# Token-stationary merge blocks with a transpose back, and delays counted from the moment of adding, in a one-core decoder trunk

## The chip, the cores and the metric

The kernel runs on one core of a Trainium2 chip. The metric is the device time of one execution in microseconds (us). A core has TensorE (PE in the views; its weight loads are PEld), VectorE (DVE), ScalarE (ACT), GpSimd (POOL) and SyncE (SP). SP issues nearly all DMAs, POOL a few. Each has its own queue of instructions; a wait holds back all that stands behind it in that queue.

## The reference, cut to what matters

D_MODEL is 2048, there are 256 tokens and one layer. The layer is `h = x + Mixer(RMSNorm(x))`, then `h = h + SwiGLU(RMSNorm(h))`, then a last norm. The part that the change touches is the end of the mixer:

```
branch_a = (o * jax.nn.silu(r)) @ w_o_gla
...
u = jax.nn.silu(_layernorm(u, conv_norm_g, conv_norm_b))
branch_b = u @ w_pw2 + b_pw2
g_a, g_b = jnp.split(gates, 2, axis=-1)
merged = jax.nn.sigmoid(g_a) * branch_a + jax.nn.sigmoid(g_b) * branch_b
return merged @ w_out
```

`gates` is a slice of the input projection `h @ w_in`, as are the conv branch's inputs, q, k, v and r. All is float32.

## The kernel before, in words

Every float32 weight is split on the fly: ACT rounds a tile to `hi` (line 194) and DVE makes `lo = raw - hi` (line 196). A product is three products of such halves. Activations are split in the same way and kept as `[128, 512]` tiles: 256 tokens of the high half beside 256 of the low half, with channels on the partitions.

The mixer is a list of blocks, each 2048 input channels by 512 output channels (`add_block`, `run_blocks`). A block has 16 input tiles of 128 (index k), handled two at a time: a chunk, so 8 chunks in a block. There are two forms for a block:

- Form M (lines 243 and 244): the weights are stationary and the tokens stream. For each k and each of four groups of 128 output channels there is one matmul of `wh` with both halves of x (512 columns) and one of `wl` with the high half (256 columns). That is 8 matmuls for each k. The result has channels on the partitions, and its two halves have to be added (`merged_sum`: an ACT copy and a DVE addition of 256 columns).
- Form A (lines 235 to 237): the tokens are stationary and the weights stream. For each k and each of two groups of 128 tokens there are three matmuls of 512 columns, 6 for each k. The result has tokens on the partitions and needs no addition.

Both forms stream 3072 columns for each k. The order of blocks is: conv values and gates (8 blocks), a small block, k and q (4), v (4, the only ones in form A), r (4), gate a `ga` (4), gate b `gb` (4), `o` (4), `pw` (4), `out` (4). Then comes the feed-forward part, which is form A throughout (lines 1248 to 1250), with its order on the engines kept as written.

The weights of chunk c+4 are cast and subtracted while chunk c is multiplied (`LOOK` is 4; there are five `hi` and `lo` buffers and three raw buffers of 1 MB). All of it comes from one list of loads on SP.

Two queues of small steps run in the background: `conv_w_` (convolution and its layer norm) and `gla_w_` (the linear attention). `pump` is called once after each chunk. It advances a counter of chunks (`tick`) and issues steps while a budget lasts, `gla_w_` first. A step may carry a delay in chunks, which is counted from the queue's last step. `drain` issues whatever is still missing.

SBUF comes from pools. `pers` holds the scaled inputs `xs`, then the merged tiles `mgs`, then in the feed-forward part the residual `htk` and the hidden tiles `hsh` and `hsl`. `apool` and `tpool` serve the mixer. They are closed just ahead of the first `out` block and their space is opened again as `fpool` and `xpool`. At the start of each `out` block, `out_before` issues two loads of the residual `xr`, 256 KB each, on SP; the end of the block adds them (line 728).

At the very start, the first block takes eight single k, each with a 256 KB weight load and a 128 KB load of x.

Of the kernel before, what the change touches and what calls it, by code (L numbers as in the profile page):

```python
# [8 lines left out]
F32 = mybir.dt.float32  # L9
F32R = mybir.dt.float32r  # L10
# [14 lines left out]
LOOK = 4  # L25
RAW = 3
NA = 44
NPERS = 16
NF = 39
NX = 6  # L30

# [10 lines left out]
def trunk(ctx: ExitStack, tc, xT, par, convw, ws, wal2, nfin, out):  # L42
# [25 lines left out]
        return tpool.tile([P, T], F32, tag="t", name=nm(s))  # L68

    def ptile(dt=F32, s="p"):  # L70
        return pers.tile([P, NB], dt, tag="p", name=nm(s))

    def misc(shape=(P, 512)):
        return pacc.tile(list(shape), F32, tag="acc", name=nm("m"))
# [39 lines left out]
    class Work:  # L114
# [3 lines left out]
            self.steps, self.last = deque(), 0  # L118

        def add(self, cost, fn, delay=0):  # L120
            self.steps.append((cost, fn, delay))

        def mark(self, name):
# [32 lines left out]

    blocks = []

    def add_block(width, nk, form, xs, evac, before=None, budget=BUD):
        blocks.append(dict(width=width, nk=nk, form=form, xs=xs, evac=evac,  # L160
                           before=before, budget=budget))

    loads = []
    staged = {}
# [38 lines left out]
    def run_blocks():  # L203
        group = 0
        for b in blocks:
            b["first"] = len(loads)
            kp = 2 * NB // b["width"]
            b["chunks"] = [(k, kp) for k in range(0, b["nk"], kp)]
            if b is blocks[0]:
                b["chunks"] = [(k, 1) for k in range(NS)] + b["chunks"][NS // 2:]  # L210
            for k, kp in b["chunks"]:
                at = k * b["width"]
                loads.append((group + at // (4 * NB), at % (4 * NB), kp * b["width"], k, kp, b["width"]))
            group += b["nk"] * b["width"] // (4 * NB)
        for b in blocks:
            if b["before"]:
                b["before"]()
            nch = len(b["chunks"])
            nt = b["width"] // P if b["form"] != "A" else 2
            acc = {}  # L220

            def part(c, n):
                hi, lo = staged[b["first"] + c]
                if c == 0:
                    acc[n] = pacc.tile([P, NB], F32, tag="acc", name=nm("acc"))
                a = acc[n]
                k0, kp = b["chunks"][c]
                for kk in range(kp):
                    k = k0 + kk
                    st, en = k == 0, k == b["nk"] - 1  # L230
                    x = b["xs"]()[k]
                    if b["form"] == "A":
                        xh, xl = x[n] if isinstance(x, list) else (
                            x[:, i * T + n * P:i * T + (n + 1) * P] for i in range(2))
                        pe.matmul(a, lhsT=xh, rhs=hi[:, kk, :], start=st, stop=False)  # L235
                        pe.matmul(a, lhsT=xh, rhs=lo[:, kk, :], start=False, stop=False)  # L236
                        last = pe.matmul(a, lhsT=xl, rhs=hi[:, kk, :], start=False, stop=en)  # L237
                    else:
                        xh, xl = x[:, 0:T], x[:, T:2 * T]
                        wh = hi[:, kk, n * P:(n + 1) * P]  # L240
                        wl = lo[:, kk, n * P:(n + 1) * P]
                        if b["form"] == "M":
                            pe.matmul(a, lhsT=wh, rhs=x, start=st, stop=False)  # L243
                            last = pe.matmul(a[:, T:2 * T], lhsT=wl, rhs=xh, start=False, stop=en)  # L244
                        else:
                            a1 = a[:, 0:T]
                            pe.matmul(a1, lhsT=wh, rhs=xh, start=st, stop=False)
                            pe.matmul(a1, lhsT=wh, rhs=xl, start=False, stop=False)
                            last = pe.matmul(a1, lhsT=wl, rhs=xh, start=False, stop=en)
                order["p"] = last.ins  # L250
                if c == nch - 1:
                    b["evac"](n, acc.pop(n))

            for c in range(nch):
                while nload[0] + halves[0] <= b["first"] + c + LOOK:
                    load_next()
                for n in range(nt):
                    part(c, n)
                del staged[b["first"] + c]
                pump(b["budget"])  # L260
# [69 lines left out]

    def x_scaled(k):
        def f():
            s = ptile(F32R, "xs")
            t = ttile("xn")
            v.scalar_tensor_tensor(t, in0=xp[k // 2][:, k % 2, :], scalar=pcol(P_MIX, k), in1=rstd,
                                   op0=ALU.mult, op1=ALU.mult)
            split(s, t)
            X.append(s)
        return f
# [336 lines left out]


    SGA, SGB = {}, {}
    MG = {}
    XR = {}  # L680
    H2 = {}
    Y2 = []
# [2 lines left out]
    HTK = {}  # L685
    sums = {}

    def o_evac(blk):
        def f(n, a):
            i = 4 * blk + n  # L690
            t = merged_sum(a)
            g = SGA[i // 2][:, i % 2, :]
            v.tensor_tensor(g, t, g, op=ALU.mult)
        return f

    def pw_evac(blk):
        def f(n, a):
            i = 4 * blk + n
            t = merged_sum(a, pcol(P_PB, i))
            u = ttile("mg")  # L700
            v.tensor_tensor(u, t, SGB[i // 2][:, i % 2, :], op=ALU.mult)
            w = ttile("mg2")
            v.tensor_tensor(w, u, SGA[i // 2][:, i % 2, :], op=ALU.add)
            MG[i] = ptile(F32R, "mgs")
            split(MG[i], w)
        return f

    def out_before(blk):
        def f():
            if blk == 0:  # L710
                mx.close()
                es = ctx.enter_context
                ffn["f"] = es(tc.tile_pool(name="fpool", bufs=NF, reuse_waits="tile"))
# [347 lines left out]
    def back(blk, n, x):  # L1061
# [7 lines left out]
            later(0.7, lambda: cut(m), 0.2)  # L1069

        def cut(m):
            hi, lo = HSV[blk, n] = ptile(F32R, "hsh"), ptile(F32R, "hsl")
            cast(hi, m)
            sub(lo, m, hi)
            if blk not in HORDER[:2]:
# [23 lines left out]
    def h2_turn(th, nb):  # L1099
        def f():  # L1100
            m = misc()
            for q in range(4):
                i = 4 * nb + q
                kp(pe.transpose(m[:, q * P:(q + 1) * P], H2[i // 2][:, i % 2, th * P:(th + 1) * P], ident))
            HTK[th, nb] = ptile(s="htk")
            kp(sc.copy(HTK[th, nb], m))
        return f

# [180 lines left out]
    rk = pair_evac(SR, AF.Silu, "sr", after=lambda h: (gla_out(h), gla_gate(h)))  # L1289
    for blk in range(4):  # L1290
        add_block(NB, KT, "M", xx, rk(blk))
    ga = pair_evac(SGA, AF.Sigmoid, "sga")
    for blk in range(4):
        add_block(NB, KT, "M", xx, ga(blk), before=layernorm if blk == 0 else None)
    gb = pair_evac(SGB, AF.Sigmoid, "sgb")
    for blk in range(4):
        add_block(NB, KT, "M", xx, gb(blk))
    for blk in range(4):
        add_block(NB, KT, "M", lambda: OG, o_evac(blk),
                  before=(lambda: gla_w_.drain(("gla", 3))) if blk == 0 else None, budget=BO)  # L1300
    for blk in range(4):
        add_block(NB, KT, "M", lambda: US, pw_evac(blk),
                  before=(lambda: conv_w_.drain("conv")) if blk == 0 else None)
    for blk in range(4):
        add_block(NB, KT, "M", lambda: MG, out_evac(blk), before=out_before(blk))
    g0[0] = sum(b["nk"] * b["width"] for b in blocks) // (4 * NB)
    run_blocks()
    run_ffn()
# [59 lines left out]
```

## Time and profile before

| | us |
|---|---|
| median of 3 runs | 1654.43 |
| lowest and highest of the 3 | 1652.99, 1657.53 |
| the profiled execution | 1652.06 |
| its span, first to last instruction | 1650.3 |
| PE busy in the span | 1635.4 |
| DVE busy | 1397.8 |
| ACT busy | 930.4 |

The profile is one execution apart from the three runs. Its span is 1.8 us shorter than its own time. Busy time of PE counts matmuls whose ends are modelled and which overlap, so the pace of PE is read from when matmuls start, not from how long one lasts.

### The profile page before, as it was taken

The page shows a single profiled execution, that of the slowest core. Times are in us where ns is not written, and L with a number is a line of the kernel's source. Part 1 is how long each engine was busy: PE and PEld are TensorE (multiplying, and loading weights), DVE is VectorE, ACT ScalarE, POOL GpSimd, SP SyncE. Part 2 cuts the span into 40 slices and gives each one's busy share as a digit, 9 for nine tenths or more (in the row PEclk, how much of TensorE's full clock was granted, in tenths as well). Part 3 has the DMA queues.
Part 4 walks back from the last instruction along what each step waited for, and adds up shares of the span by engine and source line. Part 5 has one row for each costly group of instructions (what it writes and reads, how often), then busy time and mean ns, then how long its engine had stood idle before and what let it go on. Part 6 is the DMA issues. An engine that isn't in the chain of part 4 may idle for free.

```text
span 1650.3 us, 22488 instructions
## 1 busy us (share of the span) xinstructions
PE 1635.4 (99%) x8397; PEld 1391.0 (84%) x8397; DVE 1397.8 (85%) x2104; ACT 930.4 (56%) x1276; POOL 23.9 (1%) x46
## 2 busy tenths in 40 slices
PE   9999999999999999999999999999999999999997
PEld 8888888888888888888888788888888888888886
DVE  7998999888888889887668878888888899788876
ACT  6654444666667655476445565555555555454554
POOL 0000000000000000000000000000000000000000
PEclk9999999999999999999999999999999999999999
DMA  8555545554454445545555456666666666886963
GB/s 292 197 194 194 182 185 195 181 179 176 179 179 158 175 179 180 194 163 208 199 193 210 159 192 218 228 230 230 229 229 224 219 222 218 298 286 218 322 227 113
DMA packets 78365, 340.54 MB, mean 206 GB/s; under 512 B 8976, under 2 KB 10256, under 8 KB 58160
## 3 DMA queue, kind: packets, MB, share of 16 engines
q1 hardware_dynamic: 75232, 329.61, 57.2%
q0 software_dynamic: 2880, 9.44, 1.7%
q8 instruction: 65, 1.06, 0.3%
q14 instruction: 44, 0.36, 0.1%
q10 hardware_dynamic: 144, 0.07, 0.0%
HBM read 327.54 MB, written 11.53 MB: 205 GB/s over the span
## 4 chain that ended last, share of the span: by engine, by line
PE 96%; DVE 2%; ACT 1%; DMA 1%; issue 0%; SPq 0%; ACTq 0%; DVEq 0%
PE acc L243 32%; PE acc L244 16%; PE m L1249 13%; PE m L1250 13%; PE m L1248 13%; PE acc L235 2%; PE acc L237 2%; PE acc L236 2%; DVE lo L826 1%; PE m L1068 1%; DMA xr<-in_xT_dram 0%; PE m L596 0%; PE m L511 0%; DMA x<-in_xT_dram 0%; PE m L633 0%
## 5 line engine op out<-in xcount | busy, mean ns | idle before, releaser
L194 ACT CAST hi<-raw 128x1024 fp32r<-128x1024 f32 (+1 forms) x326 | 338.9, 1041 | 343.9 <-PE acc L243 287.8
L196 DVE TENSOR_TENSOR lo<-raw,hi 128x1024 fp32r<-128x1024 f32 (+1 forms) x326 | 394.3, 1210 | 110.3 <-ACT hi L194 107.7
L243 PE MATMUL acc<-xs,hi 128*128 128x512 f32 x1280 | 452.4, 398 | 0.0
L826 DVE TENSOR_TENSOR lo<-raw,hi 128x1024 fp32r<-128x1024 f32 x264 | 317.9, 1222 | 80.3 <-ACT hi L823 79.8
L244 PE MATMUL acc<-xs,lo 128*128 128x256 f32 x1280 | 359.0, 280 | 0.0
L823 ACT CAST hi<-raw 128x1024 fp32r<-128x1024 f32 x264 | 270.6, 1050 | 155.4 <-PE m L1250 81.9
L243 PEld LDWEIGHTS acc<-xs,hi 128*128 128x128 f32 x1280 | 240.3, 188 | 57.9 <-issue 0.3
L244 PEld LDWEIGHTS acc<-xs,lo 128*128 128x128 f32 x1280 | 241.8, 189 | 0.1
L393 DVE SCALAR_TENSOR_TENSOR yc<-u,cw,yc 128x255 f32<-128x255 f32 (+14 forms) x480 | 200.4, 467 | 0.1
L1248 PE MATMUL m<-hi,y2s 128*128 128x512 f32 x404 | 158.9, 393 | 1.6 <-ACT hi L823 1.6
L1249 PE MATMUL m<-lo,y2s 128*128 128x512 f32 x404 | 157.4, 390 | 0.8 <-DVE lo L826 0.8
L1250 PE MATMUL m<-hi,y2s 128*128 128x512 f32 x404 | 157.4, 390 | 0.0
L243 PE MATMUL acc<-xu,hi 128*128 128x512 f32 x256 | 90.9, 399 | 2.2 <-DVE xu L107 2.2
L1248 PEld LDWEIGHTS m<-hi,y2s 128*128 128x128 f32 x404 | 75.9, 188 | 17.3 <-ACT hi L823 2.1
L243 PE MATMUL acc<-ogs,hi 128*128 128x512 f32 x256 | 89.9, 395 | 0.0
L1249 PEld LDWEIGHTS m<-lo,y2s 128*128 128x128 f32 x404 | 75.9, 188 | 16.2 <-DVE lo L826 1.1
L1250 PEld LDWEIGHTS m<-hi,y2s 128*128 128x128 f32 x404 | 75.8, 188 | 15.9
L243 PE MATMUL acc<-us,hi 128*128 128x512 f32 x256 | 88.8, 391 | 0.0
L243 PE MATMUL acc<-mgs,hi 128*128 128x512 f32 x256 | 88.8, 391 | 0.0
L1249 PE MATMUL m<-lo,hr 128*128 128x512 f32 x216 | 84.2, 390 | 0.7 <-DVE lo L826 0.7
L1248 PE MATMUL m<-hi,hr 128*128 128x512 f32 x216 | 84.0, 389 | 0.0
L1250 PE MATMUL m<-hi,hr 128*128 128x512 f32 x216 | 84.0, 389 | 0.0
(256 smaller groups left out, 2790.6 us busy)
## 6 DMA issues: line engine op xcount, KB each, us to landing
raw<-in_weights_dram SPq DMA_DIRECT2D x157, 1024.0 KB, 4.8
raw<-in_weights_dram SPq DMA_DIRECT2D x268, 512.0 KB, 4.9
hr<-hsd SPq DMA_DIRECT2D x56, 256.0 KB, 6.5
hsd<-hsh POOLq DMA_DIRECT2D x18, 256.0 KB, 2.6
hsd<-hsl POOLq DMA_DIRECT2D x18, 256.0 KB, 3.0
raw<-in_weights_dram SPq DMA_DIRECT2D x8, 256.0 KB, 4.9
xr<-in_xT_dram SPq DMA_DIRECT2D x8, 256.0 KB, 5.4
out_dram<-fin SPq DMA_DIRECT2D x8, 256.0 KB, 3.1
```

What stands on the lines that cost most here:

```text
L194: order["a"] = sc.copy(fl(hi), r).ins
L196: order["v"] = v.tensor_tensor(fl(lo), r, fl(hi).bitcast(F32), op=ALU.subtract).ins
L235: pe.matmul(a, lhsT=xh, rhs=hi[:, kk, :], start=st, stop=False)
L236: pe.matmul(a, lhsT=xh, rhs=lo[:, kk, :], start=False, stop=False)
L243: pe.matmul(a, lhsT=wh, rhs=x, start=st, stop=False)
L244: last = pe.matmul(a[:, T:2 * T], lhsT=wl, rhs=xh, start=False, stop=en)
L393: v.scalar_tensor_tensor(y[:, d:T], in0=u_tile(i)[:, 0:T - d], scalar=cw[:, i, CW - 1 - d:CW - d], in1=y[:, d:T], op0=ALU.mult, op1=ALU.add)
L823: kp(sc.copy(dst, src))
L826: kp(v.tensor_tensor(dst, src, hi.bitcast(F32), op=ALU.subtract))
L1248: kp(pe.matmul(a, lhsT=xh, rhs=wh, start=st, stop=False))
L1249: kp(pe.matmul(a, lhsT=xh, rhs=wl, start=False, stop=False))
L1250: kp(pe.matmul(a, lhsT=xl, rhs=wh, start=False, stop=en))
```

## The change

The 16 blocks `ga`, `gb`, `o` and `pw` go from form M to form A, so their results have tokens on the partitions.

- `sg_evac`: the sigmoid of a gate is taken by ACT straight from the accumulator, 512 columns at a time, two instructions for a block instead of four groups of three.
- `o_evac`: one DVE multiplication of 512 columns for each token group.
- `pw_evac`: the bias now runs along the columns, so it is loaded as a tile that is the same on all partitions (`BP`, one 256 KB load on SP for each `pw` block). The source is a small DRAM tile `brow`, which one POOL DMA fills at the start of the program: 2048 values are read from the packed parameters with the two dimensions exchanged. DVE then adds the bias, multiplies by gate b and adds the gated branch a.
- `turn_merged`: `out` needs channels on the partitions. For each `pw` block, two groups of four 128x128 PE transposes are put into `gla_w_`, each with an ACT copy and a DVE subtraction of 512 columns that split the result into a pair of `mgs` tiles.
- `Work.add`: when the queue is empty, its first step's delay is counted from the moment of adding.
- `out_before` of the first `out` block runs ahead of its seventh chunk (`late`) and not ahead of the block, since the mixer's pools are still needed by the transposes.
- `pers` has 8 tiles of twice the size instead of 16; `xs`, `mgs`, `htk` and the pair of hidden halves are cut from them.

```
-NPERS = 16
+NPERS = 8
...
+        return pers.tile([P, 2, NB], dt, tag="p", name=nm(s))
+    pair_of = {}
+    def phalf(i, dt=F32, s="p"):
+        if i % 2 == 0:
+            pair_of[s] = ptile(dt, s)
+        return pair_of[s][:, i % 2]
...
         def add(self, cost, fn, delay=0):
+            if not self.steps:
+                self.last = tick[0]
             self.steps.append((cost, fn, delay))
...
             for c in range(nch):
+                if c == nch - 2 and b["late"]:
+                    b["late"]()
...
+    class Merged(dict):
+        def __missing__(self, k):
+            gla_w_.drain(("mg", k // 4))
+            return self[k]
+    MG = Merged()
+    BP = {}
+    brow = dpool.tile([16, P], F32, tag="brow", name="brow")
+    with nc.allow_non_contiguous_dma(reason="2048 values once"):
+        nc.gpsimd.dma_start(brow, par[:, P_PB:P_PB + 16].rearrange("p i -> i p"))
+    def sg_evac(store):
+        def mk(blk):
+            def f(n, a):
+                store[n, blk] = atile([P, NB], s="sg")
+                sc.activation(store[n, blk], a, AF.Sigmoid)
...
     def o_evac(blk):
         def f(n, a):
-            i = 4 * blk + n
-            t = merged_sum(a)
-            g = SGA[i // 2][:, i % 2, :]
-            v.tensor_tensor(g, t, g, op=ALU.mult)
+            g = SGA[n, blk]
+            v.tensor_tensor(g, a, g, op=ALU.mult)
+    def pw_before(blk):
+        def f():
+            if blk == 0:
+                conv_w_.drain("conv")
+            BP[blk] = atile([P, NB], s="bp")
+            nc.sync.dma_start(BP[blk], brow[4 * blk:4 * blk + 4, :].rearrange("a b -> (a b)").partition_broadcast(P))
     def pw_evac(blk):
         def f(n, a):
-            i = 4 * blk + n
-            t = merged_sum(a, pcol(P_PB, i))
-            u = ttile("mg")
-            v.tensor_tensor(u, t, SGB[i // 2][:, i % 2, :], op=ALU.mult)
-            w = ttile("mg2")
-            v.tensor_tensor(w, u, SGA[i // 2][:, i % 2, :], op=ALU.add)
-            MG[i] = ptile(F32R, "mgs")
-            split(MG[i], w)
+            u = SGB[n, blk]
+            t = atile([P, NB], s="mg")
+            v.tensor_tensor(t, a, BP[blk], op=ALU.add)
+            v.tensor_tensor(u, t, u, op=ALU.mult)
+            v.tensor_tensor(u, u, SGA[n, blk], op=ALU.add)
+            if n == 1:
+                for z in range(2):
+                    turn_merged(blk, z)
+                gla_w_.mark(("mg", blk))
+    def turn_merged(blk, z):
+        st = {}
+        def t():
+            m = st["m"] = misc()
+            for j in range(2):
+                for n in range(2):
+                    pe.transpose(m[:, (2 * j + n) * P:(2 * j + n + 1) * P],
+                                 SGB[n, blk][:, (2 * z + j) * P:(2 * z + j + 1) * P], ident)
+        def cut():
+            mg = ptile(F32R, "mgs")
+            m = st["m"].rearrange("p (k t) -> p k t", k=2)
+            sc.copy(mg[:, :, 0:T], m)
+            v.tensor_tensor(mg[:, :, T:2 * T], m, mg[:, :, 0:T].bitcast(F32), op=ALU.subtract)
+            for j in range(2):
+                MG[4 * blk + 2 * z + j] = mg[:, j]
+        gla_w_.add(0.0, t, 1 if z else 3)
+        gla_w_.add(0.7, cut, 1)
...
             if blk == 0:
+                gla_w_.drain(("mg", 3))
                 mx.close()
...
-    ga = pair_evac(SGA, AF.Sigmoid, "sga")
+    ga, gb = sg_evac(SGA), sg_evac(SGB)
     for blk in range(4):
-        add_block(NB, KT, "M", xx, ga(blk), before=layernorm if blk == 0 else None)
-    gb = pair_evac(SGB, AF.Sigmoid, "sgb")
+        add_block(NB, KT, "A", xx, ga(blk), before=layernorm if blk == 0 else None)
     for blk in range(4):
-        add_block(NB, KT, "M", xx, gb(blk))
+        add_block(NB, KT, "A", xx, gb(blk))
     for blk in range(4):
-        add_block(NB, KT, "M", lambda: OG, o_evac(blk),
+        add_block(NB, KT, "A", lambda: OG, o_evac(blk),
...
-        add_block(NB, KT, "M", lambda: US, pw_evac(blk),
-                  before=(lambda: conv_w_.drain("conv")) if blk == 0 else None)
+        add_block(NB, KT, "A", lambda: US, pw_evac(blk), before=pw_before(blk))
     for blk in range(4):
-        add_block(NB, KT, "M", lambda: MG, out_evac(blk), before=out_before(blk))
+        add_block(NB, KT, "M", lambda: MG, out_evac(blk), **{"before" if blk else "late": out_before(blk)})
```

## Rows read from the trace of the kernel before

**Rows 1.** The page's span, busy times, and the granted TensorE clock in 40 slices.
```profile
span 1650.3 us, 22488 instructions
PE 1635.4 (99%) x8397; PEld 1391.0 (84%) x8397; DVE 1397.8 (85%) x2104; ACT 930.4 (56%) x1276; POOL 23.9 (1%) x46
...
PEclk9999999999999999999999999999999999999999
```

**Rows 2.** The page's chain that ended last, shares by engine.
```profile
PE 96%; DVE 2%; ACT 1%; DMA 1%; issue 0%; SPq 0%; ACTq 0%; DVEq 0%
```

**Rows 3.** Waits of PE, whole span: us in total, times, longest.
```profile
PE acc L243 <- DVE xu L107: 2.2, 2, 1.2
PE m L1248 <- ACT hi L823: 1.6, 1, 1.6
PE m L1249 <- DVE lo L826: 1.5, 2, 0.8
```

**Rows 4.** One source line's matmuls in a stretch: count, ns each, first and last start.
```profile
L243 PE MATMUL acc<-xs,hi x199: 395/398/403, 591.7 to 661.7; 128*128 128x512 f32 x199
...
L243 PE MATMUL acc<-xs,hi x68: 391/391/478, 557.9 to 583.9; 128*128 128x512 f32 x68
...
L235 PE MATMUL acc<-hi,xs x63: 389/389/397, 288.8 to 331.0; 128*128 128x512 f32 x63
```

**Rows 5.** Matmuls of line 243 by the tile they read: stages o, pw, out.
```profile
L243 PE MATMUL acc<-ogs,hi x256: 391/391/582, 664.5 to 754.4; 128*128 128x512 f32 x128
...
L243 PE MATMUL acc<-us,hi x256: 391/391/391, 754.8 to 843.2; 128*128 128x512 f32 x128
...
L243 PE MATMUL acc<-mgs,hi x256: 391/391/391, 843.5 to 931.9; 128*128 128x512 f32 x128
```

**Rows 6.** Timeline of PE in stage o: start, duration, line.
```profile
698.08 0.40 PE L243 MATMUL acc<-ogs,hi 128*128 128x512 f32 x1
...
698.44 0.59 PE L428 MATMUL m<-lf,ones 128*128 128x256 f32 x2
```

**Rows 7.** Timeline of PE around four transposes in the feed-forward part.
```profile
960.09 0.39 PE L1250 MATMUL m<-hi,dy 128*128 128x512 f32 x1
960.32 0.60 PE L1104 MATMUL m<-ident,h 128*128 128x128 f32 x4
960.67 0.48 PE L1248 MATMUL m<-hi,y2s 128*128 128x512 f32 x1
...
961.22 0.39 PE L1250 MATMUL m<-hi,y2s 128*128 128x512 f32 x1
```

**Rows 8.** Windows at the start: length, busy us by engine, granted clock, DMA share, GB/s.
```profile
4.00:18.20 14.20, 13.22 (x66) 11.37 (x65) 10.62 (x26) 7.51 (x16) 0.00 (x0) 1.00 0.95 312
18.20:21.00 2.80, 1.61 (x10) 1.14 (x9) 1.69 (x3) 2.48 (x4) 0.00 (x0) 1.00 0.86 340
```

**Rows 9.** DMA queue of the parameters from 0 to 8 us: packets, MB, share of 16 engines.
```profile
q10 hardware_dynamic: 144, 0.07, 2.8%
```

**Rows 10.** The page's DMA queues, whole span, same columns.
```profile
q1 hardware_dynamic: 75232, 329.61, 57.2%
```

**Rows 11.** The tile xr: its loads, and DMA issue to landing (min/median/max).
```profile
L717 SPq DMA_DIRECT2D xr<-in_xT_dram x8: 423/426/543, 849.2 to 927.7; - x8
...
DMA to landing us min/median/max: 5.0/5.4/6.0
```

**Rows 12.** Windows of stages gb and pw: columns as in Rows 8.
```profile
571.00:664.00 93.00, 93.00 (x537) 81.10 (x536) 83.82 (x152) 52.46 (x78) 0.00 (x0) 1.00 0.50 181
...
754.00:843.00 89.00, 89.00 (x515) 78.50 (x514) 60.73 (x90) 44.05 (x62) 0.00 (x0) 1.00 0.53 194
```

**Rows 13.** Instructions on the tiles ogs and htk, and the page's group of `lo`.
```profile
L107 DVE TENSOR_TENSOR ogs<-og,ogs x16: 417/420/426, 509.5 to 604.5; 128x256 fp32r<-128x256 f32 x16
...
L1114 DVE TENSOR_TENSOR htk<-m,htk x10: 414/684/692, 1522.2 to 1642.2; 128x512 f32<-128x512 f32 x6, 128x256 f32<-128x256 f32 x4
...
L196 DVE TENSOR_TENSOR lo<-raw,hi 128x1024 fp32r<-128x1024 f32 (+1 forms) x326 | 394.3, 1210 | 110.3 <-ACT hi L194 107.7
```

More of the change, by code (lines that the diff above doesn't have):

```diff
@@ L70, in ptile @@
     def ptile(dt=F32, s="p"):
-        return pers.tile([P, NB], dt, tag="p", name=nm(s))
+        return pers.tile([P, 2, NB], dt, tag="p", name=nm(s))
[4 more added lines that the diff above has]
+        return pair_of[s][:, i % 2]
     def misc(shape=(P, 512)):
@@ L157, in trunk, with add_block @@
     blocks = []
-    def add_block(width, nk, form, xs, evac, before=None, budget=BUD):
+    def add_block(width, nk, form, xs, evac, before=None, budget=BUD, late=None):
         blocks.append(dict(width=width, nk=nk, form=form, xs=xs, evac=evac,
-                           before=before, budget=budget))
+                           before=before, budget=budget, late=late))
     loads = []
@@ L332, in f @@
         def f():
-            s = ptile(F32R, "xs")
+            s = phalf(k, F32R, "xs")
             t = ttile("xn")
@@ L678, in trunk @@
     SGA, SGB = {}, {}
-    MG = {}
     XR = {}
@@ L686, in trunk @@
     sums = {}
+    class Merged(dict):
[12 more added lines that the diff above has]
+                sc.activation(store[n, blk], a, AF.Sigmoid)
+            return f
+        return mk
     def o_evac(blk):
         def f(n, a):
-            i = 4 * blk + n
-            t = merged_sum(a)
-            g = SGA[i // 2][:, i % 2, :]
-            v.tensor_tensor(g, t, g, op=ALU.mult)
+            g = SGA[n, blk]
+            v.tensor_tensor(g, a, g, op=ALU.mult)
+        return f
+    def pw_before(blk):
[4 more added lines that the diff above has]
+            nc.sync.dma_start(BP[blk], brow[4 * blk:4 * blk + 4, :].rearrange("a b -> (a b)").partition_broadcast(P))
         return f
@@ L1071, in cut @@
         def cut(m):
-            hi, lo = HSV[blk, n] = ptile(F32R, "hsh"), ptile(F32R, "hsl")
+            hs = ptile(F32R, "hs")
+            hi, lo = HSV[blk, n] = hs[:, 0], hs[:, 1]
             cast(hi, m)
@@ L1104, in f @@
                 kp(pe.transpose(m[:, q * P:(q + 1) * P], H2[i // 2][:, i % 2, th * P:(th + 1) * P], ident))
-            HTK[th, nb] = ptile(s="htk")
+            HTK[th, nb] = phalf(nb, s="htk")
             kp(sc.copy(HTK[th, nb], m))
```

## The prediction, made before the changed kernel had run

> **What bounds the kernel now.** I read the page first, then the chain, the waits of PE, and the pace of PE stage by stage. PE is busy 1635.4 of 1650.3 us, at a granted clock of 9 tenths or more (the 2.4 GHz level) in all 40 slices [rows 1]. The chain that ended last is 96% PE [rows 2]. PE's idle time has two places: 2.2 us near the start, waiting for the scaled input `xu`, and some 3 us in the feed-forward part for a weight's `hi` and `lo` [rows 3]. So the time is the number of matmuls by the pace at which PE starts them, plus those waits. Making an evacuation on ACT or DVE cheaper is worth nothing by itself; it only matters where PE waits.
>
> The pace is read from the first and the last start of a group [rows 4, 5]. Here the reader is to see that form M has two paces. In `gb` 199 pairs start over 70.0 us: 70.0/198 = 353.5 ns for a pair (512 and 256 columns). In `pw` 256 pairs start over 88.4 us, and in `out` the same: 88.4/255 = 346.7 ns. The median duration of the 512-column matmul tells the two apart as well, 398 ns at the slower pace and 391 at the faster; by it the 68 pairs from 557.9 to 583.9 us are at the faster one. The clock is full in both, and the pace turns at an inserted matmul: in `o` a pair takes 0.36 us up to the two matmuls of line 428 at 698.44 [rows 6], after which the rest of `o` is at the faster one. I can't say what sets it.
>
> Form A has one pace: 63 triples over 42.2 us, 42.2/62 = 680.6 ns [rows 4].
>
> **The change, part by part.**
>
> *Form A in 16 blocks.* For each k, form M takes four pairs: 1414 ns at the slower pace, 1387 at the faster. Form A takes two triples: 1361 ns. The columns are the same (3072), the matmuls 8 against 6. So a k gains 53 or 26 ns.
> - `ga` and `gb`, 128 k: some 17 at the faster pace (68 pairs), 111 at the slower: 17 x 26 + 111 x 53 = 6.3 us.
> - `o`, 64 k: slower up to 698.4, which is 33.9/0.3535 = 96 pairs or 24 k, then 40 faster: 1.3 + 1.0 = 2.3 us.
> - `pw`, 64 k at the faster pace: 1.7 us.
>
> Together 10.3 us. The bounds are 256 x 26 = 6.7 (all at the faster pace) and 256 x 53 = 13.6 (all at the slower); I take the middle because it is what the profiled execution did.
>
> *Transposes.* There are 8 groups of four, all on PE. Around such a group line 1250 starts at 960.09 and again, three matmuls later, at 961.22 [rows 7]: 1.13 us against 3 x 0.227 = 0.68. A group costs 0.45 us, eight cost 3.6 us. Do they wait? They are issued two chunks after their block, 5.4 us. In that time DVE has to do three operations of 512 columns for the second token group, near 0.69 us each, and two `lo` of 1.21 us [rows 13]; that is 4.5 us, so they find their data. If DVE were later still, PE would stand at the transposes and everything behind them; DVE has 28 of 89 us free in `pw` [rows 12].
>
> The rule of the Trainium skill, "TensorE: Matmul & The Clock Gate", section "Back-to-back issue gap", speaks against the change: a matmul takes its columns at 2.4 GHz plus about 2.5 ns. By it a pair would take 325 ns and a triple 647, form A would gain only 5 ns for each k, 1.3 us in all, and 32 transposes at 56 ns would take 1.8 us back: a loss of 0.5 us where the rows give a gain of 6.7. The rows differ from it (346.7 and 680.6 ns), and the rows decide.
>
> *The pace of `out`.* It stays in form M, now behind form A and with two groups of transposes inside. It may keep 346.7 ns or go to 353.5: 256 x 6.8 ns = 1.7 us. `r`, which follows the form A blocks of `v`, and `o` after the inserted matmuls say one each; I take half, 0.9 us, with bounds 0 and 1.7.
>
> *The bias in DRAM.* One POOL DMA at the start moves 2048 single values. No row shows such a transfer. If each is a packet of its own, each of 16 DMA engines gets 128. The start is paced by DMA: from 4 to 18.2 us the engines are 95% busy and idle 0.7 us, and PE then idles in the next stretch [rows 8], so engine time added there moves PE by as much. The nearest row is the queue that carries the parameters, 512 bytes a row: 2.8% of 16 engines over 8 us is 3.6 us for 144 packets, 25 ns each [rows 9]. That gives 128 x 25 = 3.2 us, less the idle 0.7: 2.5 us. A line through this and the main queue (201 ns for a mean of 4381 bytes [rows 10]) comes to about 5 ns at 4 bytes, 0.6 us, which fits into the idle time: 0. A packet of 4 bytes lies between; I take 1.25 us, with bounds 0 and 2.5. The Trainium skill, "DMA: Bandwidth & Descriptors", section "Rules for kernel authors", says that a strided last dimension becomes one descriptor for each element; no row here shows it.
>
> *What costs nothing.* The evacuations get cheaper: DVE is 83.8 of 93 us busy in `gb` [rows 12] and loses its additions there, so faster blocks don't starve. `BP`, four loads of 256 KB on SP, have a block (22 us) to land against some 5 to 6 us for a load of that size [rows 11]. The delay counted from adding moves the attention's steps by one chunk, 2.8 us; they end at 605 us and `o` begins at 664 [rows 13, 5]. The late `xr`: up to now the first is issued at 849.2, 5.7 us after `out` begins [rows 11, 5]; now two chunks ahead of its use, or 5.5 us, against a landing of 5.0 to 6.0. DVE may wait a little at line 728, and behind it stand the other evacuations and the `lo` of later chunks, for which PE waits. Those are four chunks, 11 us, ahead, so a wait up to that is covered; beyond it each us counts. Pairs in `pers` hold the same bytes.
>
> *Sum.* -10.3 + 3.6 + 0.9 + 1.25 = -4.6 us: 1652.06 becomes 1647.5 for a profiled execution. The median of the three runs is 2.4 us above it; from there, 1654.43 - 4.6 = **1649.8**. What a measurement of this kernel can tell from no change is about 0.3%, 5.0 us, so the forecast stands just inside "same".
>
> **The rivals.**
>
> *The timed runs are at the slower pace throughout.* They are 1 to 5.5 us above the profiled one, and 7 ns on the mixer's form M pairs would explain it. Then form A gives 13.6: -13.6 + 3.6 + 0.9 + 1.25 = -7.9, 1646.6. Against it: only one execution has a trace.
>
> *The faster pace throughout.* Then form A gives 6.7, and `out` can only lose: -6.7 + 3.6 + 1.7 + 1.25 = -0.2, 1654.3. The profiled `ga` and `gb` speak against it. The skill's rule above would end here too.
>
> *The single values cost more.* The place is the first 18 us, before the ninth k, where raw weights and x arrive just in time. The gain without the copy is 5.8 us, so from (5.8 + 0.7)/128 = 51 ns a packet the change loses, and from 90 ns it loses more than 5 us. At 100 ns the start is 12.1 us later: +6.3, 1660.7. For it: that no row shows one, and that a read and a write in DRAM both belong to it. Against it: 512 bytes take 25 ns.
>
> **How the numbers follow.** The forecast 0.62 (between -6.7 and -2.1 by the bounds; a third of it below -5.0), the slower pace 0.20, the faster pace 0.08, a dear copy 0.10, of which 0.07 is more than 5 us slower. Faster by over 0.3%: 0.20 + 0.22 = 0.42. Slower: 0.07. Within: 0.51. The range goes from the slower pace with no cost at the start and none in `out` (-13.6 + 3.6 = -10.0, 1644.5) to the faster pace and the cheap end of a dear copy, 1655.5.
>
> **What would show it.** Pairs gone in `ga` to `pw`, triples there at 680 ns; eight groups of four transposes at 0.45 us with no wait ahead of them; `out` at 346.7 or 353.5 ns; POOL's queue with some 2000 small packets ahead of 20 us, and PE's wait for `xu` grown by 0 to 2.5 us. Wrong would be: triples slower than 680 ns under the conv work, a wait of PE at the transposes or at the first chunks of `out`, weights late behind `BP` or `xr` on SP, or a start later by more than 3 us.

## The result, and the profile after

The changed kernel takes 1663.07 us (median of 4 runs, 1661.61 to 1665.16), against 1654.04 (1652.99 to 1657.53) for the kernel before, the three runs of the table and one more: a ratio of 1.0059, 95% interval 1.0043 to 1.0075. It is slower, by about 9 us; 1649.8 was forecast. The profiled execution took 1661.61 us. The page of the changed kernel, its span, busy times and granted clock in 40 slices:

```profile
span 1659.9 us, 21313 instructions
...
PE 1635.4 (99%) x7917; PEld 1372.9 (83%) x7917; DVE 1376.4 (83%) x2016; ACT 908.2 (55%) x1188; POOL 25.3 (2%) x47
...
PEclk7999999999999999999999999999999999999999
```

Against [rows 1] the span is 9.6 us longer with 480 matmuls fewer. PE's busy sum, 1635.4, happens to be the same: as overlapping matmuls are counted in full, it says little about the pace. The one digit that changed is the first slice of the granted clock. The waits of PE in the changed kernel point to the same place (us in total, times, longest):

```profile
PE acc L253 <- DVE xu L115: 11.7, 2, 6.0
PE m L1310 <- DVE lo L886: 1.4, 2, 0.8
PE m L1309 <- ACT hi L883: 1.4, 1, 1.4
```

The wait for `xu` grew from 2.2 [rows 3] to 11.7 us; the other two differ by 0.2 us at most. Windows at the start of the changed kernel (columns as in [rows 8]):

```profile
4.00:18.20 14.20, 4.68 (x17) 3.59 (x15) 1.64 (x4) 1.02 (x2) 0.00 (x0) 0.68 0.95 69
18.20:21.00 2.80, 0.59 (x1) 0.50 (x2) 1.67 (x5) 1.79 (x4) 0.00 (x0) 0.50 0.90 319
21.00:40.00 19.00, 19.00 (x96) 16.39 (x95) 16.25 (x36) 11.63 (x23) 0.00 (x0) 0.86 0.86 274
```

The last two columns are the point. Between 4 and 18.2 us the DMA engines are 95% busy, exactly as in [rows 8], but move 69 GB/s where they moved 312. The DMA queue of POOL from 0 to 20 us, and the issues from 0 to 60 us (KB each, us from issue to landing):

```profile
q0 software_dynamic: 48, 0.01, 6.8%
```

```profile
raw<-in_weights_dram SPq DMA_DIRECT2D x8, 256.0 KB, 8.4
...
x<-in_xT_dram SPq DMA_DIRECT2D x8, 128.0 KB, 10.1
...
brow<-in_par_dram POOLq DMA_DIRECT2D x1, 8.0 KB, 17.1
```

The copy into `brow` lands after 17.1 us. In its own queue it hardly shows: 48 packets, 6.8% of the engines' time. It shows in the queue that it holds up: the first eight weight loads take 8.4 us and the loads of x 10.1. The same view of the kernel before:

```profile
raw<-in_weights_dram SPq DMA_DIRECT2D x8, 256.0 KB, 4.9
...
x<-in_xT_dram SPq DMA_DIRECT2D x8, 128.0 KB, 4.7
```

What PE does with what arrives late (timeline of PE, the changed kernel: start, duration, line, and in brackets the idle time before):

```profile
11.77 0.80 PE L253 MATMUL acc<-xu,hi 128*128 128x512 f32 x1 [6.02 <-DVE xu L115]
...
20.41 0.80 PE L253 MATMUL acc<-xu,hi 128*128 128x512 f32 x1 [5.72 <-DVE xu L115]
...
21.22 0.63 PE L253 MATMUL acc<-xu,hi 128*128 128x512 f32 x1
...
26.31 0.39 PE L253 MATMUL acc<-xu,hi 128*128 128x512 f32 x1
```

Four pairs, a second wait of 5.7 us, and then matmuls of 0.63 us (the granted clock is 0.50 in 18.2 to 21 us, the 1.2 GHz level) until 26 us, when they take 0.39 again. In all, thirteen pairs run so. In the kernel before, the first five do, up to 9.9 us, as this line of its timeline shows, and there the granted clock reads 1.00 [rows 8]:

```profile
7.54 0.63 PE L243 MATMUL acc<-xu,hi 128*128 128x512 f32 x1
```

So at the start the length of a matmul tells more than the granted clock.

The later stages, by the tile that the matmuls read (first and last start), then the transposes and the late loads `xr`, each from the changed kernel:

```profile
L245 PE MATMUL acc<-hi,ogs x128: 389/389/580, 671.1 to 758.4; 128*128 128x512 f32 x128
```

```profile
L245 PE MATMUL acc<-hi,us x128: 389/389/481, 759.1 to 848.3; 128*128 128x512 f32 x128
```

```profile
L253 PE MATMUL acc<-mgs,hi x256: 389/398/478, 849.0 to 939.9; 128*128 128x512 f32 x128
```

```profile
786.05 0.39 PE L247 MATMUL acc<-hi,us 128*128 128x512 f32 x1
786.28 0.60 PE L754 MATMUL m<-ident,sg 128*128 128x128 f32 x4
786.64 0.48 PE L245 MATMUL acc<-hi,us 128*128 128x512 f32 x1
...
787.19 0.40 PE L247 MATMUL acc<-hi,us 128*128 128x512 f32 x1
```

```profile
L777 SPq DMA_DIRECT2D xr<-in_xT_dram x8: 422/428/589, 860.7 to 935.6; - x8
...
  DMA xr<-in_xT_dram: 0.7, 1
```

Stage `o` now takes 759.1 - 671.1 = 88.0 us against 90.3 in [rows 5]. A group of transposes stands in the stream with no idle time before it: 787.19 - 786.05 = 1.14 us where three matmuls take 0.68, so 0.46. `out` has the 398 ns of the slower pace where [rows 5] has 391. DVE waits 0.7 us once for `xr`, PE never.

Stage by stage, from the start of a stage's first main matmul to that of the next, in the two profiled executions:

| stage | before, us | after, us | difference |
|---|---|---|---|
| span's start to the end of the first 4 blocks | 99.1 | 111.5 | +12.4 |
| conv, k, q, v, r | 371.5 | 371.5 | 0.0 |
| `ga`, `gb` | 193.9 | 188.1 | -5.8 |
| `o` | 90.3 | 88.0 | -2.3 |
| `pw` | 88.8 | 89.9 | +1.1 |
| `out` | 88.8 | 91.3 | +2.6 |
| feed-forward, to the last matmul | 709.2 | 710.4 | +1.3 |
| sum | 1641.4 | 1650.7 | +9.3 |

The 1.3 us in the feed-forward part are no work of the change. After the two waits near its start PE ran at the lower level for a while: the granted clock is 0.50 from 955 to 958 us here, where before it stayed at 1.00 after waits of about the same length (2.2 us here, 2.4 before). In the experiments below this part takes 710.1 to 710.7 us in the six executions that have such a stretch, two of them of the kernel before with something added, and 708.5 to 709.0 in the eight that have none.

### The profile page after: what moved, and what is told of

Same layout as the page of the kernel before. It is cut to its first block, busy times and chain, and to the rows that moved or that the text cites. A ratio compares the mean times of both kernels' runs of the same rounds, so it can differ in the third digit from the quotient of the medians.

```text
span 1659.9 us, 21313 instructions
## 1 busy us (share of the span) xinstructions
PE 1635.4 (99%) x7917; PEld 1372.9 (83%) x7917; DVE 1376.4 (83%) x2016; ACT 908.2 (55%) x1188; POOL 25.3 (2%) x47
## 4 chain that ended last, share of the span: by engine, by line
PE 95%; DVE 2%; DMA 2%; ACT 1%; issue 0%; SPq 0%; ACTq 0%; DVEq 0%
PE acc L253 18%; PE m L1310 13%; PE m L1311 13%; PE m L1309 13%; PE acc L254 9%; PE acc L245 9%; PE acc L247 9%; PE acc L246 9%; DMA raw<-in_weights_dram 1%; DVE lo L886 1%; PE m L1128 1%; DMA xr<-in_xT_dram 0%; PE m L608 0%; PE m L523 0%; PE m L646 0%
## 5 line engine op out<-in xcount | busy, mean ns | idle before, releaser
L253 PE MATMUL acc<-xs,hi 128*128 128x512 f32 x768 | 270.3, 397 | 0.0
L254 PE MATMUL acc<-xs,lo 128*128 128x256 f32 x768 | 215.4, 281 | 0.0
L253 PEld LDWEIGHTS acc<-xs,hi 128*128 128x128 f32 x768 | 144.1, 188 | 34.9 <-issue 0.3
L245 PE MATMUL acc<-hi,xs 128*128 128x512 f32 x384 | 151.3, 394 | 0.0
L247 PE MATMUL acc<-hi,xs 128*128 128x512 f32 x384 | 149.5, 389 | 0.0
L246 PE MATMUL acc<-lo,xs 128*128 128x512 f32 x384 | 149.5, 389 | 0.0
L254 PEld LDWEIGHTS acc<-xs,lo 128*128 128x128 f32 x768 | 145.1, 189 | 0.0
L253 PE MATMUL acc<-xu,hi 128*128 128x512 f32 x256 | 93.4, 407 | 11.7 <-DVE xu L115 11.7
L245 PEld LDWEIGHTS acc<-hi,xs 128*128 128x128 f32 x384 | 72.1, 188 | 15.3 <-issue 0.7
## 6 DMA issues: line engine op xcount, KB each, us to landing
x<-in_xT_dram SPq DMA_DIRECT2D x8, 128.0 KB, 10.1
```

## The experiments

Theory: the copy of single values holds up the loads at the start and is the whole loss. Rivals: that it is POOL's queue or a DRAM-to-DRAM copy as such; that new work on SP or PE later on is the cause.

**The copy, later.** The changed kernel with the copy issued on POOL behind the first mask of the attention, at 336 us.

```
             sel = nc.gpsimd.affine_select(...)
+            if h == 0:
+                with tc.issue_after(sel.ins), ...:
+                    nc.gpsimd.dma_start(brow, par[:, P_PB:P_PB + 16].rearrange("p i -> i p"))
```

> The changed kernel with the copy of the 2048 bias values issued behind the first attention block's mask on POOL, near 330 us, and not at the start. Theory (the copy at the start takes the DMA engines from the first weights and x): the start is that of the kernel before, 12.4 us earlier than in the changed kernel, so 1663.1 - 12.4 = 1650.7 us; the weights of that later stretch are four chunks ahead and cover the copy, at worst some us of waiting there. Rival 1 (the start is late for another reason, such as the layout of the pools): 1663 us. Rival 2 (the copy costs PE its 12 us wherever it stands): near 1663 us, with the waits moved to 330 us.

1648.14 us, ratio 0.9976 (0.9964 to 0.9989). The copy holds up the loads there too, but nobody waits. A window of this kernel while the copy runs, and the same window of the kernel without a copy (the third experiment):

```profile
340.00:350.00 10.00, 10.00 (x46) 8.29 (x45) 8.06 (x14) 6.85 (x10) 0.00 (x0) 1.00 0.12 13
...
340.00:350.00 10.00, 10.00 (x46) 8.29 (x45) 8.03 (x13) 6.84 (x11) 0.00 (x0) 1.00 0.31 110
```

The DMA engines move 13 GB/s for 10 us, where they move 110 without the copy. The weight load of 1 MB issued at 343.5 us took 11.7 us to land, the one in its place without the copy 4.8. PE is busy all 10 us in both: its weights are four chunks ahead. The copy took 14.4 us to land.

**The copy alone, in the kernel before.** Nothing reads it.

```
+    brow = dpool.tile([16, P], F32, tag="brow", name="brow")
+    with nc.allow_non_contiguous_dma(reason="2048 values once"):
+        nc.gpsimd.dma_start(brow, par[:, P_PB:P_PB + 16].rearrange("p i -> i p"))
```

> The kernel before, with nothing added but the copy at the start. Theory: the start is 12.4 us later, 1654.0 + 12.4 = 1666.4 us. Rival (the copy hurts only together with the rest of the change): 1654 us.

1668.17 us, ratio 1.0085 (1.0070 to 1.0100). The waits of PE in it:

```profile
PE acc L243 <- DVE xu L107: 18.1, 2, 11.1
```

The copy landed after 23.4 us, the first four blocks ended at 118.4 instead of 99.1, and every later stage of the mixer is as long as before. The profiled execution is the slowest of the four runs (1664.76 to 1672.98 us). So the copy alone makes the kernel slower, more than the whole change does, which also gains something.

**No copy.** The bias comes as an input of its own, and `BP` is loaded from it.

```
-            nc.sync.dma_start(BP[blk], brow[4 * blk:4 * blk + 4, :]...partition_broadcast(P))
+            nc.sync.dma_start(BP[blk], bpw[blk * NB:(blk + 1) * NB].partition_broadcast(P))
```

> The changed kernel without the copy: the bias vector comes as an input of its own and each block's tile is loaded from it. Theory: as with the copy moved, 1650.7 us, which is 3.3 us (0.2%) below the kernel before: form A gives 8.1 us in three stages, the transposes take 3.6 and the pace of out 1.7 of it back, and pw gains 1.7. Rival (form A and the transposes cancel out, and what the trace shows as a gain is spread of one execution): 1654 us.

1648.26 us, ratio 0.9972 (0.9961 to 0.9984). The mixer's stages from conv to `out` are those of the changed kernel to 0.1 us; the start is 11.5 us shorter (100.0 against 111.5) and the feed-forward part 2.0, as its clock stayed up. What is left of the change is a gain: 5.6 us by the medians, 4.6 by the ratio (2.6 to 6.5).

**The same bytes in runs of 64.** Also on POOL, also from DRAM to DRAM, 8 KB.

```
-        nc.gpsimd.dma_start(brow, par[:, P_PB:P_PB + 16].rearrange("p i -> i p"))
+    nc.gpsimd.dma_start(brow.rearrange("a (b i) -> (a b) i", i=16), par[:, P_PB:P_PB + 16])
```

> The changed kernel with a copy at the same place, on the same queue and of the same 8 KB from the same parameters, but in 128 runs of 64 bytes instead of 2048 of 4 bytes; the bias that pw adds is then in a wrong order. Theory (the price is that of each single value): the start is within 1 us of the kernel before, 1651 us. Rival (a DRAM to DRAM copy on POOL at the start is dear as such): the start stays late, 1663 us.

1649.27 us, ratio 0.9972 (0.9962 to 0.9981). Its first window:

```profile
4.00:18.20 14.20, 12.34 (x65) 10.66 (x64) 10.60 (x26) 8.00 (x17) 0.00 (x0) 0.88 0.97 318
```

318 GB/s again, and a landing after 4.0 us. So it isn't a copy on POOL as such, nor a copy within DRAM: it is how the 8 KB are cut. Single values sent from another queue were not tried.

**Half of the values, and an eighth.** Does each value have its price?

```
-    brow = dpool.tile([16, P], F32, tag="brow", name="brow")
+    brow = dpool.tile([16, 64], F32, tag="brow", name="brow")
...
+        nc.gpsimd.dma_start(brow, par[0:64, P_PB:P_PB + 16].rearrange("p i -> i p"))
```

> The changed kernel with half the copy: 1024 single values in 16 rows of 64; pw then adds the first half of the bias twice. Theory (a price for each value): the copy lands in about half of 17.1 us and the start is late by about 6 us instead of 12, near 1655 us. Rival (a fixed price of starting such a copy): still 17 us to land, 1661 us.

One run, 1658.81 us, with a wait for `xu` of 11.2 us; beside 1653.08 for the kernel before, a ratio of 1.0035, without an interval. With 16 in place of 64:

> The changed kernel with a copy of 256 single values (16 for each of 16 rows) in place of 2048; the bias is these 256 values, repeated, so it is not the reference's. 2048 values made PE wait 11.7 us for xu, 1024 values 11.2 us, and no single values 2.7 us. Theory (each value has its price): an eighth of the values is an eighth of the added wait, (11.7 - 2.7)/8 = 1.1, so a wait of 3 to 5 us, a landing below 8 us, and about 1650 us. Rival (the half copy cost as much as the whole one because the price is that of having such a copy at the start at all): a wait near 11 us and about 1659 us.

1656.08 us, ratio 1.0018 (1.0007 to 1.0030), a wait of 6.6 us. It lies between the two expectations: an eighth of the values costs about half of the loss. The price isn't proportional to the number of values.

**Pairs, and the order.** First 1024 runs of 8 bytes with the parameter's row outermost.

```
+        nc.gpsimd.dma_start(brow.rearrange("(i x) (p j) -> (x p) i j", x=2, j=2),
+                            par[:, P_PB:P_PB + 16].rearrange("p (i j) -> p i j", j=2))
```

> The changed kernel with the same 8 KB copied as 1024 runs of two values (8 bytes); the bias arrives in another order, so it is not the reference's. Theory (the price goes by the run, whatever is in it): as many runs as the copy of 1024 single values, so a wait of PE for xu of 9 to 11 us and about 1659 us. Rival (the price goes by the value): as the whole copy of 2048 single values, a wait near 11.7 us or more and about 1663 us. A third reading, that only single values are dear: a wait near 2.7 us and 1649 us, as with runs of 64 bytes.

1651.54 us, ratio 0.9986 (0.9975 to 0.9997), a wait of 3.9 us: much less than 1024 single values. As two things had changed, two more runs: the single values with only the order changed (the copy's result is the same), and the pairs in the old order.

```
+        nc.gpsimd.dma_start(brow.rearrange("i p -> p i"), par[:, P_PB:P_PB + 16])
```

> The changed kernel with the same 2048 single values and the same result of the copy, but the two dimensions of the transfer exchanged: the parameter's row is outermost, so that values read one after the other are neighbours and values written one after the other are 512 bytes apart. Theory (the order is dear, not the 4 bytes): PE's wait for xu at 3 to 5 us, a landing below 8 us, and about 1650 to 1652 us, as with the 1024 pairs. Rival (a run of 4 bytes is dear in any order): a wait of 9 us or more and about 1660 to 1663 us.

> The changed kernel with 1024 runs of 8 bytes in the order of the changed kernel's copy: the output index outermost, so that runs written one after the other are neighbours. The bias arrives in another order, so it is not the reference's; the outermost dimension is 8 and not 16. Theory (the order is dear): a wait for xu of 9 us or more and about 1659 us, as with 1024 single values. Rival (only the 4 bytes are dear): a wait of 3 to 5 us and about 1651 us, as with pairs in the other order.

1656.36 us, ratio 1.0017 (1.0008 to 1.0027), and 1654.58 us, ratio 1.0001 (0.9990 to 1.0011). Neither reading alone holds: exchanging the order takes about 7 us off the single values, and doubling the run about 10 us off in the old order and 5 in the other. Between the two orders of pairs the 2.5 us are at the edge of the noise. All copies side by side; the last column is the ratio less the 0.9972 of the kernel without a copy, times 1654 us. Each ratio with an interval is known to 0.001 to 0.0016 either way, so an added time to 2 or 3 us. Landing and wait are of one execution each, and the change's own copy landed after 23.4 us in the kernel before:

| copy | runs x bytes | landing, us | PE's wait for `xu`, us | ratio | added, us |
|---|---|---|---|---|---|
| none | | | 2.9 | 0.9972 | 0 |
| whole rows | 128 x 64 | 4.0 | 2.7 | 0.9972 | 0 |
| pairs, by row | 1024 x 8 | 6.6 | 3.9 | 0.9986 | 2.3 |
| pairs, old order | 1024 x 8 | 10.6 | 6.0 | 1.0001 | 4.8 |
| values, by row | 2048 x 4 | 12.9 | 9.5 | 1.0017 | 7.4 |
| 256 values, old order | 256 x 4 | 9.4 | 6.6 | 1.0018 | 7.6 |
| 1024 values, old order | 1024 x 4 | 13.9 | 11.2 | 1.0035 | 10.4 |
| the change | 2048 x 4 | 17.1 | 11.7 | 1.0059 | 14.4 |

**The delay counted from adding.** The kernel without a copy, with the edit of `Work.add` undone.

```
         def add(self, cost, fn, delay=0):
-            if not self.steps:
-                self.last = tick[0]
             self.steps.append((cost, fn, delay))
```

> The kernel with the bias as its own input, with the other half of the change undone: delays are again counted from the queue's last step, not from the moment of adding. Theory (the attention's steps have 60 us to spare, and the transposes find their data even two chunks earlier, or PE waits a few tenths of a us for them four times): 1648.3 us, within 1. Rival (the transposes then stand at the end of their block and PE waits for three DVE operations, about 2 us, four times): 1656 us.

1665.40 us, ratio 1.0084 (1.0067 to 1.0101), far more than either expectation. Waits of PE, and its timeline at the end of the first `pw` block, in this kernel:

```profile
PE m L749 <- DVE sg L734: 10.9, 4, 2.8
```

```profile
768.09 0.39 PE L245 MATMUL acc<-hi,us 128*128 128x512 f32 x1
771.16 0.33 PE L749 MATMUL m<-ident,sg 128*128 128x128 f32 x1 [2.68 <-DVE sg L734]
```

```profile
798.00:804.00 6.00, 6.00 (x23) 4.87 (x22) 2.23 (x3) 1.63 (x2) 0.00 (x0) 0.75 0.11 42
```

The queue had been empty for many chunks, so a delay counted from its last step had long run out: the transposes are issued right behind the block, and PE stands 2.7 us until DVE has done its three operations for both token groups. That happens at each of the four blocks, 10.9 us, and behind the second, third and fourth of these waits the granted clock falls as well (0.75 in the window above, 0.74 from 822 to 828 us, 0.50 from 853 to 855). `pw` takes 104.9 us instead of 89.9.

**No transposes.** The kernel without a copy and without the 32 transposes; `out` multiplies the untransposed data.

```
-            m = st["m"] = misc()
...
-                    pe.transpose(m[:, ...], SGB[n, blk][:, ...], ident)
+            st["m"] = SGB[z, blk]
```

> The kernel with the bias as its own input, without the 32 transposes: the split reads the merged tile with tokens on the partitions, so out gets untransposed data. Theory (a group of four costs 0.45 us): pw is shorter by 6 x 0.45 = 2.7 us, 87.2 us, and out by 0.9 at the same pace, or by 2.6 if the transposes inside out are what put it at the slower pace. Rival (the slower pace comes from form A ahead of it, as in r): out 90.4 us.

One run, 1645.29 us. `pw` takes 87.04 us instead of 89.89 and `out` 90.44 instead of 91.32, 3.7 us in all: 0.47 for each of 8 groups. `out` still has the slower pace, so the transposes in it are not needed for that. Form A ahead of it isn't enough either: in the kernel with the old `Work.add` `out` follows form A too, and there it has the faster pace, 74.2/214 = 346.7 ns a pair:

```profile
L251 PE MATMUL acc<-mgs,hi x215: 392/392/395, 865.7 to 939.9; 128*128 128x512 f32 x108
```

**Can the pace be set?** Small matmuls of ones, 1 to 3 of 16 to 128 columns, were put ahead of 19 blocks of form M; then two of 16 columns ahead of seven chosen blocks; then the same ahead of 13 blocks of the kernel before.

```
+            d = misc()
+            for _ in range(2):
+                with tc.issue_after(order["p"]):
+                    order["p"] = pe.matmul(d[:, 0:16], lhsT=ones, rhs=ones[:, 0:16], start=True, stop=True).ins
```

> The kernel with the bias as its own input, with one to three small matmuls of ones into an unused bank put ahead of 19 form M blocks, of 16 to 128 columns. Theory (the pace of form M, 346.7 or 353.5 ns a pair, is a matter of how the stream of matmuls and weight loads came to stand, and a matmul in between can turn it): some blocks change their pace against the run without them, each by 64 x 4 x 6.7 ns / 4 = 0.43 us for a block of 64 pairs, less about 0.1 to 0.5 us for each inserted one. Rival (the pace is set by what else runs, or by the tiles): every block keeps its pace.

> The kernel with the bias as its own input, with two matmuls of 16 columns into an unused bank ahead of seven form M blocks: the second, third, first of k, first, second and fourth of r, second of out. Theory (two small matmuls in a row bring form M to its faster pace from either, and it stays there until others come in between): k and q or the conv blocks gain 1.7 to 2.6 us, r 1.0, out 1.3, less 7 x 0.1: about 3.5 us below the 1648.3 without them, 1644.8 us. Rival (the paces seen with single matmuls were chance): 1648 us.

> The kernel before, all form M, with the same two small matmuls ahead of thirteen blocks: the second, third, first of k, first, second and fourth of r, the four of gate a, the first two of gate b, the first of o. Theory (more than a third of what form A gained is the slower pace of form M, which can be had without form A): gate a and b gain up to 3, o 0.6, k and q 1.7, r 1.0, less 1.3: about 5 us below 1653.9, 1649 us. Rival (no change): 1654 us.

The first, one run: 1652.31 us. Against the kernel without a copy the conv blocks went from 353 to 349 ns a pair and the k and q blocks from 347 to 356, the inserted matmuls included. But the changed kernel has 347 and 353 there with nothing inserted (see *The paces* below), so this run doesn't show that the inserted matmuls did it. The second: 1647.73 us, ratio 0.9963 (0.9951 to 0.9976). It beats both kernels, but its interval doesn't tell it from the kernel without a copy; by the traces its last matmul begins 2.4 us sooner. Behind the inserted matmuls `out` has the faster pace, 65.2/188 = 346.8 ns a pair, against 67.8/192 = 353.1 without them:

```profile
L262 PE MATMUL acc<-mgs,hi x189: 392/395/395, 859.7 to 924.9; 128*128 128x512 f32 x189
...
L253 PE MATMUL acc<-mgs,hi x193: 395/398/403, 859.9 to 927.7; 128*128 128x512 f32 x193
```

The third: 1658.05 us, ratio 1.0026 (1.0017 to 1.0035), slower than untouched. The k and q blocks are at the faster pace (346.9 ns), but from conv to `gb` the time is the same (565.6 us against 565.4), so the inserted matmuls took what the pace gave. Here `o` began at the faster pace, the matmuls of line 428 in its middle turned it to the slower one (before, they turned it to the faster, [rows 6]), and `pw` kept that. The pairs of `pw` in this kernel:

```profile
L252 PE MATMUL acc<-us,hi x256: 394/399/404, 757.4 to 847.5; 128*128 128x512 f32 x128
```

So inserted matmuls do turn the pace: behind the pairs of 16 columns it was the faster one, and with those of line 428 the way depends on what it was. What sets it is not settled.

## Why the prediction was wrong, point by point

*The step that failed is "The bias in DRAM".* It took 1.25 us with a bound of 2.5; the start measured +12.4 us in the profiled execution, and the added time by the medians is about 14. The bound was no bound: it took 25 ns, the time of a 512-byte packet in [rows 9], as the most that a 4-byte value could cost. If the 128 values of one engine went one after the other, a landing of 17.1 us makes 17.1/128 = 134 ns for each. The same division of the 256 values gives 9.4/16 = 588 ns, so no one price for each value fits. The way from copy to loss was as the text had it: the start is paced by the loads, [rows 8], and what holds them up there moves PE. The rival "The single values cost more" was the right one, at a chance of 0.10. At 100 ns it put the start 12.1 us later, close to the 12.4 measured, but the 100 ns was an example and taken from no row, so that match is luck. Its model, a price for each value, did not hold: 256 values cost 7.6 us, 2048 cost 14.4, and run length and order count too. Besides the waits, 11.7 - 2.2 = 9.5 us, the start lost some 3 us, most of it because thirteen pairs and not five ran with matmuls of 0.63 us (granted clock 0.50 from 9.2 to 26.2 us).

The prediction cited a rule on this and gave it no price. The Trainium skill, "DMA: Bandwidth & Descriptors", section "Rules for kernel authors", has a strided last dimension made into one descriptor for each element, and advises to rearrange it so that it is contiguous. The runs agree in effect (17.1 us to land in single values, 4.0 in runs of 64 bytes), but the trace records the copy as 48 packets, so one descriptor for each element is not to be seen in it.

*Form A:* forecast -10.3. Measured -5.8 in `ga` and `gb`, -2.3 in `o`, and in `pw` -1.7 (87.04 us without transposes against 88.75): -9.8 us. This step was right, at 680 ns a triple. The rule of the Trainium skill ("TensorE: Matmul & The Clock Gate", section "Back-to-back issue gap"), by which the change would lose 0.5 us, does not hold for this stream: 512 columns take 680.6/3 = 226.9 ns where it gives 215.8, and without the copy the change gains. The section gives that formula for an isolated matmul; its figure for a stream of weight loads and matmuls, about 131 ns at 512 columns, is further off still.

*Transposes:* forecast 3.6 without a wait, measured 3.7 and none. But the reason was left out. The text took "two chunks after their block" as given, and costed the counting of the delay only as a shift of the attention's steps. That edit is what keeps PE from waiting: undone, it costs about 17 us (1665.40 against 1648.26; 14.3 by the two spans). It was costed at nothing, and the work that it protects was not named.

*The pace of `out`:* half of 1.7 us was taken; it went to the slower pace, 90.44 - 88.75 = 1.7, the upper bound.

*What costs nothing:* right for the evacuations, for `BP` (landing in 5.0 us, nobody waited) and for the late `xr`. The feed-forward part's 1.3 us of lower clock was not in the sum and isn't the change's.

*The sum:* 12.4 - 9.8 + 3.7 + 1.7 + 1.3 = +9.3 us, the difference of the last matmuls. Without the copy's term the forecast would have been 1654.43 - 5.85 = 1648.6, and the kernel without a copy measured 1648.26. That this is so close is in part luck: the measured terms other than the copy's and the clock's add up to -9.8 + 3.7 + 1.7 = -4.4 us, the ratio says -4.6 and the medians -5.6.

*The paces:* neither rival about them came up as it was put. The stages from conv to `r` take 371.5 us in the kernel before, in the changed one and in the one without a copy, but that hides a change of pace inside. The conv blocks in the kernel before and in the kernel without a copy, then the k and q blocks in the same two:

```profile
L243 PE MATMUL acc<-xs,hi x249: 391/391/391, 99.8 to 185.8; 128*128 128x512 f32 x125
L253 PE MATMUL acc<-xs,hi x244: 395/398/403, 100.0 to 185.9; 128*128 128x512 f32 x122
...
L243 PE MATMUL acc<-xs,hi x244: 395/398/403, 196.8 to 282.7; 128*128 128x512 f32 x122
L253 PE MATMUL acc<-xs,hi x249: 391/391/391, 196.9 to 282.9; 128*128 128x512 f32 x125
```

Before, conv is at 86.0/248 = 346.8 ns a pair and k and q at 85.9/243 = 353.5; without a copy it is the other way round. As both have 256 pairs, the sum stays the same. Of the thirteen executions with no small matmuls put in, seven (the changed kernel among them) go one way and six (the kernel before with the copy among them) the other, and the pace at the end of the first four blocks goes with that of conv. From `r` to `pw` the kernel before has the same paces with the copy and without it, the ones that the sum had taken. Each kernel has one trace, so whether the timed runs of one kernel differ in this is open.

*Slips in the working:* the upper bound -2.1 of the forecast should read -10.3 + 3.6 + 1.7 + 2.5 = -2.5, and the line through the two queues comes to some 2 ns at 4 bytes and not 5. Neither moves the forecast. The median length of a matmul doesn't always tell the paces apart: `out` at 346.8 ns a pair has 395 above, not 391.

*What was to show it:* "some 2000 small packets" on POOL's queue never appeared, 48 did. Who had checked the forecast by that row alone would have thought the copy harmless.

## What to carry to other kernels

A small copy is priced by how it is cut, not by its bytes: move it to where the loads are ahead, or keep its runs long, and treat an operation that no row shows as unbounded until one does. Look for its cost in the landing times and the GB/s of the other queues, whatever the busy share says, not in its own row. When work that waits on another engine is put into a background queue, what its delay is counted from decides whether the bottleneck engine stands still.

## What was not expected of the hardware

- While one 8 KB copy in 4-byte runs was under way, the DMA engines moved 69 GB/s at 95% busy for 14 us (312 GB/s at 95% without it), and in mid-kernel 13 GB/s at 12% busy for 10 us (110 at 31%); 256 values (1 KB) already took 9.4 us to land. Why a few cost so much, and why the order matters, stays open.
- Waits of about the same length near 950 us left PE at 2.4 GHz in one execution (granted clock 1.00) and at 1.2 GHz in another (0.50).
- Form M's two paces, 347 and 353 ns a pair, are a state that is kept from block to block, that a few inserted matmuls can turn, and that differs, in conv and in k and q, between kernels that hold the same work there in the same order.
